# A hybrid decoder layer: x laid out by columns for the Z stage, unscaled fp32 products first, and roots spread by TensorE

## The chip, the cores and the metric

The kernel runs on one core of a Trainium2 chip. A core has five engines that run side by side, each through its own list of instructions in order: TensorE (PE in the profile; its weight loads are PEld), VectorE (DVE), ScalarE (ACT), GpSimd (POOL) and SyncE (SP), which here only starts transfers between the device memory and the on-chip memory. Matrix products land in eight accumulator banks (PSUM), from which VectorE and ScalarE read. The metric is the device time of one execution in microseconds. Three runs are shown for the kernel before; a further execution was recorded by the profiler.

## The reference, cut to what matters

One decoder layer on x of 1024 tokens by 1024 features, all in float32. The part that the change touches is the first norm and the last 520 columns of the input projection: the gate z (512 columns) and the two small inputs a and b of the delta rule (8 columns).

```python
def rms_norm(x, w):
    y = x * lax.rsqrt(jnp.mean(x * x, axis=-1, keepdims=True) + EPS)
    return y * w

h = rms_norm(x, norm1_w)
proj = h @ w_in
da_q, da_k, da_v, dn_qkv, dn_z, dn_a, dn_b = jnp.split(proj, [...], axis=-1)
...
dn_o = rms_norm(dn_o, dn_out_norm_w) * jax.nn.silu(dn_z)
...
x = x + mix @ w_out
h = rms_norm(x, norm2_w)
x = x + jnp.square(jax.nn.relu(h @ w_up)) @ w_down
```

The root of a token (one over the root mean square of its row of x) scales a whole row of h. So it can be put on a row of the product as well: (r x) W = r (x W).

## The kernel before, in words

The kernel keeps h turned, that is with features over partitions and tokens along the free axis, because a product contracts over partitions. It keeps it as two float32r tensors: `hH`, the rounded value, and `hL`, what the rounding left. A product of full precision is made of three passes of float32r (H by H, H by L, L by H); I call it a split product.

The Z stage is the first of the kernel, up to 63 us. It has eight blocks of 128 tokens and two units of 260 columns of weights (u = 0 and 1), so 16 products. For a block `tb` the steps before are:

- `z_square` (ScalarE): squares of a row of x (tokens over partitions), summed along the way; `z_root`: mean and epsilon on VectorE (L223), power -1/2 on GpSimd (L224);
- `z_scale` (L335, VectorE): x times root times norm weight, rows as they came;
- `z_turn` (L340, TensorE): eight 128 by 128 transposes into two banks;
- `h_round` (L345, ScalarE) writes `hH` out of the banks and `h_rest` (L349, VectorE) writes `hL`;
- `z_mm` (L290 to L292, TensorE): the split product with a unit, 24 matmuls of 260 columns;
- `z_gate`: tanh (L298, ScalarE), (tanh + 1) times z (L300, VectorE), times the norm weight of the gated output (L301, GpSimd), and a store from SyncE's queue (L304); the second unit also yields the eight columns a and b (L303).

The weights arrive as float32 (`wraw`) and are split by `z_round` (L308, ScalarE) and `z_rest` (L312, VectorE). The very first product, block 0 with unit 0, is made in plain fp32 from an unsplit copy `hF` (L388), since nothing is split yet. The norm weight is spread over all partitions by two products with a row of ones (L362) and copied out (L366, L369). Ahead of and between these stand twelve transposes that nobody reads (L358, L365).

Order: inside `tc.manual_schedule(engines={T, V, S})` (L352) TensorE, VectorE and ScalarE run the instructions in the order in which the program writes them. GpSimd and SyncE are ordered by a planner that simulates the program. The loop at L421 runs over blocks 2 to 7: the first product of the block, turns and splits of the next block, the gate, square, root and scaling of the block after that, the second product and its gate. What follows the stage in the text (masks, small constants, L441 to L507) is planned to issue behind the instructions collected in `mark` and the last load of x. All loads and the stores of gates go through SyncE's one queue, in order: block 0 of x in halves, block 1, the eight pieces of weights of both units, the gate's norm weight, blocks 2 to 7 of x, then the small constants and the first weights of the next stage (`load_unit`, L191).

After the Z stage come the delta rule's projections (`dn_proj`, first product at L198), the scan, attention, the output projection and the MLP. Their order on TensorE is fixed by the program.

## Time and profile before

| | us |
|---|---|
| median of 3 runs | 1255.41 |
| lowest, highest | 1255.33, 1256.09 |
| the profiled execution | 1254.91 |
| its span | 1253.2 |
| TensorE, VectorE, ScalarE, GpSimd busy | 1232.7, 817.7, 612.5, 111.4 |

The granted clock of TensorE was 0.997 over the span.

How to read the profile: all times are microseconds from the start of the span unless a row says ns. A row of the timeline has start, duration, engine, source line, operation, output<-inputs, shapes, count, and in brackets the idle time ahead of it and what ended it. A group's row ends with busy time and mean duration in ns, then the idle time before its instructions by what ended it. The chain of waits is the chain of work that ended last, followed back from the end; its rows have start, duration, engine, tile and line. A row of waits on SyncE's queue names the line that waited, what for, the total, the times and the longest. Matmuls are pipelined, so a matmul is booked longer than the distance to the next.

### The profile page before, as it was taken

The numbers are of one execution on the slowest core, as the hardware profiler recorded it, in microseconds if no ns is written. First come the engines' busy times: TensorE is split into PE (matmuls) and PEld (weight loads), VectorE is DVE, ScalarE is ACT, GpSimd is POOL, SyncE is SP. The second block draws the span as 40 slices with busy tenths as digits, with TensorE's granted clock in tenths as the row PEclk, the third lists the DMA queues.
The fourth block names the chain that finished last, engine by engine and source line by source line (L and its number), as shares of the span: only waits on it lengthen the run. The fifth ranks groups of instructions, "written<-read, shape, count | busy, mean of one in ns | idle before, by whom it ended". The sixth has DMA issues, their size and how long they took to land.

```text
span 1253.2 us, 18946 instructions
## 1 busy us (share of the span) xinstructions
PE 1232.7 (98%) x6965; PEld 1061.6 (85%) x6965; DVE 817.7 (65%) x1416; ACT 612.5 (49%) x1239; POOL 111.4 (9%) x143
## 2 busy tenths in 40 slices
PE   9999999999998999999999999999999999999998
PEld 8978888899998998787888888888888888888887
DVE  6567797656556647776589555655569855787553
ACT  5378553334345545656567445445564333333331
POOL 3311110022112200001200000000000000000000
PEclk9999999999999999999999999999999999999999
DMA  7134554368758557322255544443469655422301
GB/s 245 43 102 129 160 159 113 89 215 240 249 144 243 157 176 180 97 66 80 85 185 172 201 159 175 168 152 132 170 219 376 230 199 201 168 101 101 133 35 67
DMA packets 156343, 197.93 MB, mean 158 GB/s; under 512 B 20650, under 2 KB 110554, under 8 KB 156251
## 3 DMA queue, kind: packets, MB, share of 16 engines
q1 hardware_dynamic: 156248, 196.72, 48.4%
q8 instruction: 55, 0.90, 0.3%
q14 instruction: 38, 0.30, 0.1%
q10 hardware_dynamic: 2, 0.00, 0.0%
HBM read 131.66 MB, written 65.01 MB: 157 GB/s over the span
## 4 chain that ended last, share of the span: by engine, by line
PE 91%; DMA 4%; DVE 2%; ACT 2%; issue 1%; SPq 0%; DVEq 0%; POOL 0%; ACTq 0%; POOLq 0%
PE X L1391 5%; PE X L1392 5%; PE X L1393 5%; PE X L1691 4%; PE X L1690 4%; PE X L1689 4%; PE ps_dn L198 3%; PE ps_dn L199 3%; PE ps_dn L200 3%; PE ps_qk L955 3%; PE ps_qk L957 3%; PE ps_qk L956 3%; PE Y L1391 2%; PE Y L1392 2%; PE Y L1393 2%; PE ps_op L1220 2%
## 5 line engine op out<-in xcount | busy, mean ns | idle before, releaser
L1309 ACT CAST hH<-ur 128x1024 fp32r<-128x1024 f32 x56 | 58.9, 1051 | 173.3 <-PE Y L1690 89.8
L1310 DVE TENSOR_TENSOR hL<-ur,hH 128x1024 fp32r<-128x1024 f32 x56 | 68.3, 1223 | 79.9 <-ACT hH L1309 79.8
L955 PE MATMUL ps_qk<-wH,hH 128*128 128x256 f32 x384 | 115.5, 301 | 0.1
L957 PE MATMUL ps_qk<-wH,hL 128*128 128x256 f32 x384 | 109.1, 284 | 0.0
L956 PE MATMUL ps_qk<-wL,hH 128*128 128x256 f32 x384 | 109.0, 284 | 0.0
L1310 DVE TENSOR_TENSOR op<-raw,op 128x1024 fp32r<-128x1024 f32 x48 | 58.7, 1223 | 74.5 <-PE X L1392 41.5
L1689 PE MATMUL X<-hH 128*128 128x512 f32 x224 | 87.1, 389 | 0.0
L1690 PE MATMUL X<-hL,hH 128*128 128x512 f32 x224 | 87.1, 389 | 0.0
L1691 PE MATMUL X<-hH,hL 128*128 128x512 f32 x224 | 87.1, 389 | 0.0
L198 PE MATMUL ps_dn<-hH,wH 128*128 128x512 f32 x192 | 76.1, 397 | 0.3 <-ACT cp L574 0.3
L200 PE MATMUL ps_dn<-hH,wL 128*128 128x512 f32 x192 | 75.9, 396 | 0.0
L199 PE MATMUL ps_dn<-hL,wH 128*128 128x512 f32 x192 | 75.7, 395 | 0.0
L955 PEld LDWEIGHTS ps_qk<-wH,hH 128*128 128x128 f32 x384 | 74.0, 193 | 0.3 <-ACT qn L974 0.2
L956 PEld LDWEIGHTS ps_qk<-wL,hH 128*128 128x128 f32 x384 | 74.0, 193 | 0.0
L957 PEld LDWEIGHTS ps_qk<-wH,hL 128*128 128x128 f32 x384 | 73.8, 192 | 0.0
L193 DVE TENSOR_TENSOR wL<-wraw,wH 128x512 fp32r<-128x512 f32 x64 | 43.9, 697 | 37.9 <-ACT wH L192 37.7
L1310 DVE TENSOR_TENSOR hL<-dw,hH 128x1024 fp32r<-128x1024 f32 x56 | 68.1, 1219 | 0.5 <-ACT hH L1309 0.5
L1309 ACT CAST op<-raw 128x1024 fp32r<-128x1024 f32 x48 | 50.4, 1051 | 35.3 <-PE Y L1393 19.9
L1309 ACT CAST hH<-dw 128x1024 fp32r<-128x1024 f32 x56 | 58.7, 1048 | 10.1 <-DMA dw<-in_w_down_dram 4.4
L192 ACT CAST wH<-wraw 128x512 fp32r<-128x512 f32 x64 | 38.2, 620 | 48.7 <-DMA wraw<-in_w_units_dram 35.3
L578 DVE SCALAR_TENSOR_TENSOR cy<-cp,pv,cy 128x512 f32<-128x512 f32 x72 | 53.7, 747 | 7.2 <-ACT cy L576 6.4
L1080 DVE TENSOR_REDUCE mx<-ps_sc 128x1 f32<-128x128 f32 (+7 forms) x64 | 47.6, 754 | 15.3 <-PE ps_sc L1078 14.8
(366 smaller groups left out, 3451.3 us busy)
## 6 DMA issues: line engine op xcount, KB each, us to landing
ur<-ud SPq DMA_DIRECT2D x28, 1024.0 KB, 4.9
raw<-in_w_up_dram SPq DMA_DIRECT2D x32, 512.0 KB, 4.1
dw<-in_w_down_dram SPq DMA_DIRECT2D x32, 512.0 KB, 6.6
wraw<-in_w_units_dram SPq DMA_DIRECT2D x48, 256.0 KB, 3.9
qk_d<-qa SPq DMA_DIRECT2D x32, 256.0 KB, 3.6
ud<-ua SPq DMA_DIRECT2D x16, 512.0 KB, 3.3
ud<-s SPq DMA_DIRECT2D x16, 512.0 KB, 2.7
pka<-park_d SPq DMA_DIRECT2D x32, 192.0 KB, 3.7
```

What stands on the lines that cost most here:

```text
L198: T.matmul(ps, lh(k), rh(k), start=(k == 0), stop=False)
L199: T.matmul(ps, lh(k), rl(k), start=False, stop=False)
L200: T.matmul(ps, ll(k), rh(k), start=False, stop=(k == n - 1))
L955: T.matmul(ps[:, :256], hH[:, k, sl], wh[:, k, :], start=(k == 0), stop=False)
L956: T.matmul(ps[:, :256], hH[:, k, sl], wl[:, k, :], start=False, stop=False)
L957: T.matmul(ps[:, :256], hL[:, k, sl], wh[:, k, :], start=False, stop=(k == KB - 1))
L1309: S.copy(dst[0], src)
L1310: V.tensor_tensor(dst[1], src, dst[0].bitcast(F32), ALU.subtract)
L1391: T.matmul(ps, op[0][:, k, cs], h[0][:, k, :], start=start and k == 0, stop=False, skip_group_check=True)
L1689: T.matmul(bank[t], v[0][:, j, sl], v[2][:, j], start=s0, stop=False, skip_group_check=True)
L1690: T.matmul(bank[t], v[0][:, j, sl], v[3][:, j], start=False, stop=False, skip_group_check=True)
L1691: T.matmul(bank[t], v[1][:, j, sl], v[2][:, j], start=False, stop=s1, skip_group_check=True)
```

## The change

The host passes two more arrays: `x_cols`, x with each block of 128 tokens turned (features over partitions), and `w1_cols`, the norm weight in the same layout. x itself is still loaded, as rows, for the squares alone.

- A block of columns `xT` is weighed in place with the norm weight (`z_weigh`): blocks 0 and 1 on VectorE, blocks 2 to 7 on GpSimd, in two halves.
- The four products of blocks 0 and 1 (`z_raw`) are plain fp32 products of weighed but unscaled columns with unsplit weights. Their gates take the root as a scale: half the root inside the tanh, and the root in a second step on VectorE, which also multiplies by the gate's norm weight; that step was GpSimd's.
- A root is still a value per token on a partition. To scale columns, it has to lie along the free axis, the same on all partitions. `z_diag` puts the roots on a diagonal (VectorE), `z_spread` multiplies a matrix of ones by it (TensorE, fp32, 128 columns), and the result in a bank is multiplied onto `xT` by `z_scale` (VectorE, two halves). `hH` and `hL` are then made from `xT` in the on-chip memory.
- A spread stands inside a product, after its first two of eight steps: that of block 2 in the last unscaled product, of 3 in the first product of block 2, of 0 in the second product of block 2, of 4 in the first product of block 3, of 1 in the second of block 3, and then of each block in the first product of the one before.
- Blocks 0 and 1 are scaled and split late, after block 3, since only later stages read them.
- GpSimd now also runs in the written order. Its masks are written ahead of the stage. The transposes of normed rows, the broadcast of the norm weight and the copy `hF` are gone; ten transposes that nobody reads stand at the start.
- Tiles: six for `xT`, four for rows of x, one for squares, two for diagonals. Loads: half of `xT` 0, a piece of weights, the other half, three pieces, `xT` 1, four pieces, then `xT` and x of blocks 2 and 3, the gate's norm weight, x of blocks 0 and 1, and `xT` and x of blocks 4 to 7.

The diff, cut to its core:

```diff
+    def z_raw(tb, u, pool, tag, mid=None):
+
+        ps = pool.tile([P, 512], F32, tag=tag, name="ps_z")
+        for k in range(KB):
+            if k == 2 and mid is not None:
+                z_spread(mid)
+            T.matmul(ps[:, :UC], xTs[tb][:, k, :], wz[u][1][k // 2][:, k % 2, :], start=k == 0, stop=k == KB - 1)
+        return ps
+
+    def z_gate(tb, u, ps, raw=False):
         n = UC if u == 0 else 252
         th = n1.tile([P, UC], F32, tag="zth", name="zth", bufs=2)
-        S.activation(th[:, :n], ps[:, :n], AF.Tanh, scale=0.5)
         zg = n1.tile([P, UC], F32, tag="zg", name="zg", bufs=4)
+        r = roots[tb]
+        S.activation(th[:, :n], ps[:, :n], AF.Tanh, scale=half_r[tb] if raw else 0.5)
         last = V.scalar_tensor_tensor(zg[:, :n], th[:, :n], 1.0, ps[:, :n], ALU.add, ALU.mult)
-        G.tensor_tensor(zg[:, :n], zg[:, :n], dnw4[:, UC * u:UC * u + n], ALU.mult)
-        if u == 1:
+        w = dnw4[:, UC * u:UC * u + n]
+        if raw:
+            last = V.scalar_tensor_tensor(zg[:, :n], zg[:, :n], r, w, ALU.mult, ALU.mult)
+        else:
+            G.tensor_tensor(zg[:, :n], zg[:, :n], w, ALU.mult)
+        if u == 1 and raw:
+            last = V.tensor_scalar(ab[:, tb, :], ps[:, 252:260], r, None, ALU.mult)
+        elif u == 1:
             last = V.tensor_copy(ab[:, tb, :], ps[:, 252:260])
...
+    roots, half_r, spreads, diags = {}, {}, {}, {}
+
+    def z_weigh(tb, eng, parts=2):
         for i in range(parts):
+            c = cuts[i] if parts > 1 else slice(0, KB)
+            n = KB // parts
+            eng.tensor_tensor(xTs[tb][:, c, :], xTs[tb][:, c, :],
+                              w1c[:, c].unsqueeze(2).broadcast_to([P, n, P]), ALU.mult)
+
+    def z_root(tb):
+
+        sq = n1.tile([P, DM], F32, tag="sq", name="sq", bufs=1)
+        ss = n1.tile([P, 1], F32, tag="nss", name="nss", bufs=2)
+        S.activation(sq, xts[tb], AF.Square, accum_out=ss)
+        r = roots[tb] = n1.tile([P, 1], F32, name=f"nr{tb}")
+        rstd(r, ss, 1.0 / DM, EPS, n1, "nrt", 1)
+
+    def z_diag(tb):
+        diags[tb] = n1.tile([P, P], F32, tag="dg", name="dg", bufs=2)
+        V.tensor_scalar(diags[tb], ident, roots[tb], None, ALU.mult)
+
+    def z_spread(tb):
+
+        ps = pm.tile([P, 512], F32, tag="pm", name="ps_r")
+        marks[tb] = T.matmul(ps[:, :P], ones, diags[tb], start=True, stop=True)
+        spreads[tb] = ps[:, :P]
+
+    def z_scale(tb):
+        sl = slice(tb * P, (tb + 1) * P)
+        xT, last = xTs[tb], []
+        for c in cuts:
+            V.tensor_tensor(xT[:, c, :], xT[:, c, :], spreads[tb].unsqueeze(1).broadcast_to([P, 4, P]), ALU.mult)
+            last.append(S.copy(hH[:, c, sl], xT[:, c, :]))
+        for c in cuts:
+            last.append(V.tensor_tensor(hL[:, c, sl], xT[:, c, :], hH[:, c, sl].bitcast(F32), ALU.subtract))
         return last
...
+        for i in range(10):
             T.transpose(pw[:, 0:P], ident, ident)
+        z_weigh(0, V)
+        z = {(0, 0): z_raw(0, 0, pj, "pj")}
+        for i in range(3):
             z_round(0, i)
             z_rest(0, i)
+        z_weigh(1, V)
+        z_round(0, 3)
+        z_rest(0, 3)
+        z[1, 0] = z_raw(1, 0, pj, "pj")
+        for i in range(4):
             z_round(1, i)
             z_rest(1, i)
+        z[0, 1] = z_raw(0, 1, ph, "ph")
+        z_weigh(2, G)
         z_root(2)
+        z_diag(2)
+        z_weigh(3, G)
+        z[1, 1] = z_raw(1, 1, ph, "ph", 2)
+        z_scale(2)
         z_root(3)
+        z_diag(3)
+        z[2, 0] = z_mm(2, 0, pt_, "pt", 3)
+        G.tensor_scalar(dnw4[:, 0], dnw4[:, 0], 0.5, None, ALU.mult)
+        G.tensor_copy(dnw4[:, 1:4], dnw4[:, 0:1].broadcast_to([P, 3, P]))
+        dnw4 = dnw4.rearrange("p h e -> p (h e)")
+        for tb in range(2):
+            z_root(tb)
+            half_r[tb] = n1.tile([P, 1], F32, name=f"hr{tb}")
+            V.tensor_scalar(half_r[tb], roots[tb], 0.5, None, ALU.mult)
+            z_diag(tb)
+            if tb == 0:
+                z_scale(3)
+            for u in range(2):
+                z_gate(tb, u, z[tb, u], True)
+            if tb == 0:
+                z[2, 1] = z_mm(2, 1, pt_, "pt", 0)
+                z_weigh(4, G)
+        z_gate(2, 0, z[2, 0])
+        z_scale(0)
+        z_root(4)
+        z_diag(4)
+        for tb in range(3, NT):
+            z[tb, 0] = z_mm(tb, 0, mid=tb + 1 if tb + 1 < NT else None)
+            if tb + 2 < NT:
+                z_weigh(tb + 2, G)
             if tb + 1 < NT:
+                last = z_scale(tb + 1)
+            z_gate(tb - 1, 1, z[tb - 1, 1])
+            if tb == 3:
+                mark = [marks[4], *last]
+            z[tb, 1] = z_mm(tb, 1, mid=1 if tb == 3 else None)
+            if tb == 3:
+                z_scale(1)
+            z_gate(tb, 0, z[tb, 0])
             if tb + 2 < NT:
                 z_root(tb + 2)
+                z_diag(tb + 2)
+        z_gate(NT - 1, 1, z[NT - 1, 1])
```

More of the change, by code (lines that the diff above doesn't have):

```diff
@@ L252, in tile_hymba_layer, with z_unit @@
     ab = const.tile([P, NT, 8], F32, name="ab")
[L253 to L255 removed]
+    def z_unit():
         ops = [staged(t).rearrange("p (k c) -> p k c", k=KB) for t in ("wH", "wL")]
@@ L344, in h_round @@
[L344 to L355 removed]
+            c = cuts[i] if parts > 1 else slice(0, KB)
@@ L356, in tile_hymba_layer @@
+    G.affine_select(gt_f, ones, pattern=[[-1, P]], compare_op=ALU.is_gt, fill=0.0,
+                    base=0, channel_multiplier=1)
+    G.affine_select(blk.rearrange("p (b c) -> p b c", c=32), ones.rearrange("p (b c) -> p b c", c=32),
+                    pattern=[[-32, 4], [0, 32]], compare_op=ALU.is_ge, fill=0.0,
+                    base=-32, channel_multiplier=1)
+    marks = {}
+    with tc.manual_schedule(engines={T.engine, V.engine, S.engine, G.engine}):
         pw = pm.tile([P, 512], F32, tag="pm", name="ps_w")
-        for i in range(6):
+        for i in range(10):
```

182 lines of the change are left out of this document (48 added, 134 removed).

## The prediction

> **What bounds the kernel now.** I read the page first: the span and the busy time of each engine.
>
> ```profile
> span 1253.2 us, 18946 instructions
> PE 1232.7 (98%) x6965; PEld 1061.6 (85%) x6965; DVE 817.7 (65%) x1416; ACT 612.5 (49%) x1239; POOL 111.4 (9%) x143
> ```
>
> TensorE (PE) is busy for 98% of the span, so time can only come out of its work, or out of the first microseconds; and every microsecond in which it newly waits is lost. The change touches only the Z stage. So next came the chain of waits from 0 to 66 us, and TensorE's timeline for the stage's first and last products.
>
> ```profile
> 10.20 1.96 PE ps_z L388 x8
> 13.03 1.75 PE ps_z L388 x8
> 40.90 0.87 PE ps_tr L340 x8
> 47.52 0.87 PE ps_tr L340 x8
> 24.26 0.29 PE L290 MATMUL ps_z<-wH,hH 128*128 128x260 f32 x1
> 63.45 0.40 PE L198 MATMUL ps_dn<-hH,wH 128*128 128x512 f32 x1
> ```
>
> The chain is TensorE throughout. The one fp32 product (L388) has 16 records in 1.96 + 1.75 = 3.7 us. A block of 128 tokens lasts 47.52 - 40.90 = 6.62 us; less 0.87 us for the eight turns (L340) that leaves 5.75 us for two split products, 2.87 us each. At about 24.3 us the four products of blocks 0 and 1 are done and block 2 is turned; at 63.45 us the next stage begins. In between lie 12 split products (34.4 us), five groups of turns (4.35 us) and one small turn with the joints (0.4 us): 39.15 us, without a wait. VectorE (DVE), ScalarE (ACT) and GpSimd (POOL) are hidden under it.
>
> **The change, part by part: the front.** The first product needs no root, no scaling and no turning any more. It needs half a block of x by columns, w1_cols, one weighing instruction on VectorE and the first piece of weights. How fast pieces land is read from the queue of SyncE.
>
> ```profile
> 3.54 0.63 ACT L321 ACTIVATE hn<-xt 128x512 f32<-128x512 f32 x1 [0.90 <-DMA xt<-in_x_dram]
> 7.49 1.06 ACT L321 ACTIVATE hn<-xt 128x1024 f32<-128x1024 f32 x1 [2.61 <-DMA xt<-in_x_dram]
> 8.20 0.33 SPq L275 DMA_DIRECT2D dnw<-in_dn_out_norm_w_dram  x1
> 8.85 3.73 SPq L277 DMA_DIRECT2D xt<-in_x_dram  x6
> SPq L277 <- DMA wraw<-in_w_z_dram: 1.9, 6, 0.3
> ```
>
> The first 0.26 MB are there at 3.5 us, 1.05 MB at 7.5 us. The issue at 8.20 us and the six from 8.85 us each waited for a piece of weights, one 0.27 MB piece per 0.67 us (0.40 MB/us). Read on this scale, with an early end about 1 us ahead of it because the first pieces are smaller, the changed order lands half a block at 3.5 us, the first weights at 4.2 us, the second weight piece (1.06 MB in all) at 6.5 to 7.5 us, the fourth (1.6 MB) at 8 to 8.9 us, block 1 (2.1 MB) at 9.3 to 10.2 us, the last weights (3.2 MB) at 12 to 12.9 us. So the first product starts at about 4.3 us but is paced by weights; the second waits for block 1 and half its weighing (0.7 us) until 10.0 to 10.9 us. From there the products run on: three at 3.7 us and one spread, so four are done at 21.3 to 22.2 us. I take 21.8 us: 2.5 us ahead of 24.3 us. The 4.2 MB of x that are now loaded twice add 10.5 us of traffic at this rate. Behind them on SyncE's queue stand the small constants and the first two pieces of unit weights:
>
> ```profile
> 12.87 0.45 SPq L464 DMA_DIRECT2D rows<-in_conv_w_dram  x1
> 24.21 0.90 SPq L191 DMA_DIRECT2D wraw<-in_w_units_dram  x2
> 36.53 0.22 DVE L443 CAST identb<-ident 128x128 bf16<-128x128 f32 x1
> 61.06 1.13 ACT L192 CAST wH<-wraw 128x512 fp32r<-128x512 f32 x2
> ```
>
> They went out at 12.9 to 25 us and were used from 36 us (constants) and 61 us (unit weights). They move behind the last x, whose slot comes free when block 1 is scaled, at about 42 us; eleven issues at 0.45 us and two of weights then end near 48 us. I cost this at nothing: some 12 us of products still cover the unit weights. Without that cover ScalarE would wait for a landing, and the next stage's first product with it.
>
> **TensorE's work after that.** The five groups of turns go (-4.35 us); six spreads come. A spread is one fp32 product of 128 columns in two records; eight one-record turns took 0.87 us, so two records are about 0.22 us, 0.25 us with the change of operands: +1.5 us. From 21.8 us TensorE has 34.4 + 1.5 = 35.9 us. With the 0.4 us of small turn and joints, and without a wait, the stage would end at 58.1 us, 5.35 us earlier than before.
>
> **The waits that come.** The roots no longer scale rows ahead of the turns; each block now goes square (ACT), mean (DVE), power (POOL), diagonal (DVE), spread (PE), two scalings (DVE), two roundings (ACT), two rests (DVE). All four engines run in the order written. The spread of block 4 stands inside the first product of block 3, after six of its matmuls; but its diagonal stands on VectorE behind the scaling of block 3, the gates of blocks 0 and 1, one gate of block 2 and the whole scaling of block 0. The durations, from the groups of the Z stage (0 to 63.4 us), of GpSimd over the whole kernel, and the timeline:
>
> ```profile
> L349 DVE TENSOR_TENSOR hL<-ps_tr,hH 128x512 fp32r<-128x512 f32 x14 | 9.0, 687 | 10.8 <-ACT hH L345 10.8
> L300 DVE SCALAR_TENSOR_TENSOR zg<-zth,ps_z 128x260 f32<-128x260 f32 x8 | 3.3, 417 | 2.6 <-ACT zth L298 2.4 <-DMA zg_d<-zg 0.2
> L321 ACT ACTIVATE hn<-xt 128x1024 f32<-128x1024 f32 x7 | 7.5, 1066 | 2.6 <-DMA xt<-in_x_dram 2.6
> L345 ACT CAST hH<-ps_tr 128x512 fp32r<-128x512 f32 x14 | 7.5, 589 | 17.4 <-PE ps_tr L340 17.4
> L224 POOL TENSOR_TENSOR nr<-nrt,neghalf 128x1 f32<-128x1 f32 x8 | 4.4, 552 | 9.7 <-DVE nrt L223 9.1 <-DVE qw L473 0.7
> L1249 POOL TENSOR_TENSOR hn<-hn,w2b 128x512 f32<-128x512 f32 x4 | 5.2, 1290 | 5.5 <-ACT hn L1248 5.5
> 45.03 1.28 DVE L335 SCALAR_TENSOR_TENSOR hn<-xt,nr,w1b 128x1024 f32<-128x1024 f32 x1 [1.08 <-POOL nr L224]
> 46.24 0.41 DVE L300 SCALAR_TENSOR_TENSOR zg<-zth,ps_z 128x252 f32<-128x252 f32 x1
> 37.82 0.21 DVE L490 TENSOR_SCALAR dawb<-dawb 128x128 f32<-128x128 f32 x1
> ```
>
> One instruction follows another 0.07 us before the first is booked as ended (45.03 + 1.28 against 46.24), so a half-block pass costs VectorE 0.62 us, a gate step 0.34 us, a diagonal 0.2 us.
>
> Block 3's root comes first. The spread of block 2 is issued at about 18.3 us; two scalings and two roundings end at 20.5 us; the square of block 3 (1.07 us and 0.1 us of reading) follows on ScalarE, then mean, power (0.55 us) and diagonal, ready at 22.8 us (times on the early bound of the front). TensorE stands at that spread from 22.05 us: 0.8 us lost.
>
> From 22.8 us VectorE's list to the diagonal of block 4 is: three means, two half roots and three diagonals (1.1 us), the scaling and rests of blocks 3 and 0 (8 x 0.62 = 5.0 us), nine gate steps (3.1 us), two small copies (0.24 us): 9.4 us. It also waits, with nothing else in its order, for the power of block 0 (its square queues behind that of block 3: 1.3 us), the power of block 1 (0.7 us), a tanh (0.25 us), the square of block 4 behind block 0's roundings (0.6 us) and its power (0.7 us): 3.55 us. So the diagonal is ready at about 35.8 us. TensorE reaches the spread at 29.1 us: after 22.85 us it has the rest of one split product (0.25 + 2.1 us), one with a spread (3.1 us) and 0.7 us. It loses 6.8 us.
>
> Block 5 is next: between the two spreads VectorE has the scaling of blocks 4 and 1 and two gates, 6.1 us and 1.5 us of waits, against 6.0 us of TensorE work: 1.8 us lost. From block 6 on the list is one scaling and two gates per 5.98 us of TensorE, and it fits. Sum of the waits: 9.4 us.
>
> **GpSimd's new passes.** Weighing blocks 2 to 7 puts two 1.29 us passes per block on GpSimd. What they do to VectorE is shown by four meetings in the timeline.
>
> ```profile
> 24.09 1.27 DVE L335 SCALAR_TENSOR_TENSOR hn<-xt,nr,w1b 128x1024 f32<-128x1024 f32 x1
> 24.18 2.47 POOL L301 TENSOR_TENSOR zg<-zg,dnw 128x252 f32<-128x252 f32 x2 [1.46 <-DVE ab L303]
> 25.29 0.41 DVE L300 SCALAR_TENSOR_TENSOR zg<-zth,ps_z 128x252 f32<-128x252 f32 x1
> 36.75 0.75 POOL L301 TENSOR_TENSOR zg<-zg,dnw 128x260 f32<-128x260 f32 x1 [2.52 <-issue]
> 36.80 0.78 DVE L461 CAST caus<-caus_f 128x128 bf16<-128x128 f32 x1
> 61.71 1.85 DVE L193 TENSOR_TENSOR wL<-wraw,wH 128x512 fp32r<-128x512 f32 x2
> 61.76 1.24 POOL L301 TENSOR_TENSOR zg<-zg,dnw 128x260 f32<-128x260 f32 x1 [2.16 <-issue]
> ```
>
> Each time the later one stood until the earlier had ended: GpSimd's pair took 2.47 us instead of 1.45 us behind L335; the cast took 0.78 us instead of 0.22 us; L193 and GpSimd took turns. L300, which reads one input from PSUM, was not held. In the changed lists a weighing is issued on GpSimd straight behind the power, and the diagonal of the same block (SBUF to SBUF, like the cast) a hop later. So the diagonals of blocks 0, 4, 5 and 6 each stand behind a 1.29 us pass, and so do some rests. Lower bound 0, upper bound four times 1.23 us, 4.9 us; I take 4.8 us, since every meeting on record held.
>
> The Trainium skill, "SBUF — State Buffer", section "Who interferes with whom", has the rule: VectorE and GpSimd share one port pair that whoever issues first keeps for the whole instruction, and VectorE needs it for two SBUF inputs or for a two-port copy, cast or tensor_scalar. By that rule the sum is the one with 4.8 us, without it the one with 0; the four rows agree with it.
>
> Other edits. The gates of blocks 0 and 1 move their last multiply to VectorE (counted above). VectorE's constants (L443 to L490) still have to lie somewhere behind the scaling of block 4; 0 to 2.0 us, and I take 0, the value that the timeline of before shows. The warm-up at the start has two transposes fewer and no broadcast of the norm weights; all of it lies ahead of the first product.
>
> **Sum.** -2.5 us (front), -2.85 us (turns less spreads), +9.4 us (waits), +4.8 us (passes): +8.85 us; the stage ends at 72.3 us, and what follows, with TensorE as full as before, moves by the same. The profiled execution took 1254.9 us (span 1253.2 us), 0.5 us under the median of the runs shown, 1255.4 us; so about 1263.8 us. Below 0.2% (2.5 us) a measurement of this kernel can't tell a change from none.
>
> **Rivals.**
> A, not slower: VectorE's list runs without hand-over waits and without standing behind GpSimd. Then its 9.4 us alone count: diagonal 4 at 32.2 us, 3 us lost there, 0.8 us at block 3, none at block 5. The sum is -5.35 + 3.8 = -1.55 us, 1253.4 us; with the front's early bound 1252.9 us. It decides once all waits together stay under 5.35 us. For it: VectorE was busy for only 65%. Against: the hand-overs follow from the written order, and L335 already waited 1.08 us for a power.
> B, the passes cost nothing: -5.35 + 9.4 = +4.05 us, 1259 us. For it: no pass as wide as these meets VectorE in the Z stage of before. Against: the four rows.
> C, TensorE slows after its long wait. At the start it ran at half rate:
>
> ```profile
> 1.53 1.54 PE L358 MATMUL ps_w<-ident 128*128 128x128 f32 x6 [1.53 <-POOL ident masks.py:199]
> 11.99 1.04 PE L340 MATMUL ps_tr<-ident,hn 128*128 128x128 f32 x8
> ```
>
> Six transposes took 1.54 us early and eight 1.04 us later, 0.22 against 0.11 us apiece. If it falls back after standing for 7 to 9 us, some 3.6 us of work cost double: +1.9 us, 1265.7 us; as long as at the start (from 1.5 to 10.4 us) up to +4.4 us, 1268.2 us. Nothing before shows a wait that long. The Trainium skill, "TensorE: Matmul & The Clock Gate", Part 1, says an idle window of about 3.4 us halves the clock until as much sustained work has passed; by an estimate from that page it is the +1.9 us.
> D, the constants land in the blocks where VectorE's list is the limit: +2.0 us, 1265.8 us.
>
> **Chances.** The forecast (1261 to 1265.5 us) 0.48; A 0.15, of which 0.09 at or past its early end (faster) and 0.06 short of it (same); B 0.17; C 0.12; D 0.08. The range leaves out A: 1257 to 1269 us, from 2 us under B to past the far end of C. Faster 0.09, same 0.06, slower 0.85.
>
> **What would show it.** Right: the first Z product before 5 us; the fourth done at 21 to 22.5 us; TensorE waiting 5 to 9 us at the fourth spread, that of block 4, near 29 us; a diagonal booked with over 1 us beside a weighing; the next stage's first L198-type product at 67 to 74 us. Wrong: that product before 63 us, or a spread of block 4 that hardly waits, which would mean that VectorE's order is not the limit; or a later stage that takes the delay up.

## The result and the profile after

The changed kernel takes 1269.3 us (median of four runs, 1266.95 to 1271.39), the kernel before 1255.5 us on the same chip: 1.0109 times as long, interval 1.0087 to 1.013. The forecast was 1263.8 us, with a range of 1257 to 1269 us: slower was right, but the time lies 5.5 us above the forecast and 0.3 us above the range. The profiled execution took 1267.9 us.

From the page of the changed kernel, the lines that answer to the first ones of before:

```profile
span 1266.2 us, 18837 instructions
PE 1229.3 (97%) x6887; PEld 1058.6 (84%) x6887; DVE 827.0 (65%) x1438; ACT 614.1 (49%) x1235; POOL 119.5 (9%) x151
PEclk9799999999999999999999999999999999999999
```

TensorE has 3.4 us less work than before and the span is 13.0 us longer, so it stands still for some 16 us more. The second slice of 32 us is the only one in which the granted clock is under nine tenths. Its timeline shows the places; the number in brackets is the time without work ahead of the row and what ended it.

```profile
4.86 0.77 PE L322 MATMUL ps_z<-wraw,xT 128*128 128x260 f32 x1 [0.93 <-DMA wraw<-in_w_z_dram]
21.58 0.47 PE L311 MATMUL ps_z<-wH,hH 128*128 128x260 f32 x1
23.64 0.35 PE L375 MATMUL ps_r<-dg,ones 128*128 128x128 f32 x1 [1.00 <-DVE dg L370]
40.60 0.55 PE L375 MATMUL ps_r<-dg,ones 128*128 128x128 f32 x1 [10.55 <-DVE dg L370]
49.03 0.39 PE L311 MATMUL ps_z<-wH,hH 128*128 128x260 f32 x1 [0.87 <-DVE qw L490]
51.53 0.55 PE L375 MATMUL ps_r<-dg,ones 128*128 128x128 f32 x1 [1.52 <-DVE dg L370]
62.85 0.36 PE L311 MATMUL ps_z<-wH,hH 128*128 128x260 f32 x1 [1.11 <-DVE ab L340]
70.16 0.36 PE L311 MATMUL ps_z<-wH,hH 128*128 128x260 f32 x1 [1.11 <-DVE ab L340]
78.83 0.39 PE L198 MATMUL ps_dn<-hH,wH 128*128 128x512 f32 x1
```

The first product starts at 4.86 us and the first scaled one (block 2, unit 0) at 21.58 us. From there the stage lasts 78.83 - 21.58 = 57.25 us; I call this the scaled stretch and compare the experiments by it, since the start of the first scaled product differs by up to 1.8 us between profiles. Six waits, 16.2 us together, lie in it. The longest is the one at the spread of block 4. What VectorE did meanwhile:

```profile
23.18 0.31 DVE L370 TENSOR_SCALAR dg<-ident,nr 128x128 f32<-128x128 f32 x1 [0.67 <-POOL nr L224]
24.80 0.15 DVE L438 TENSOR_SCALAR hr<-nr 128x1 f32<-128x1 f32 x1 [1.11 <-POOL nr L224]
24.88 0.99 DVE L370 TENSOR_SCALAR dg<-ident,nr 128x128 f32<-128x128 f32 x1
31.00 0.15 DVE L438 TENSOR_SCALAR hr<-nr 128x1 f32<-128x1 f32 x1 [0.66 <-POOL nr L224]
31.75 0.42 DVE L331 SCALAR_TENSOR_TENSOR zg<-zth,ps_z 128x260 f32<-128x260 f32 x1 [0.41 <-ACT zth L330]
35.23 0.42 DVE L331 SCALAR_TENSOR_TENSOR zg<-zth,ps_z 128x260 f32<-128x260 f32 x1 [1.54 <-DMA zg_d<-zg]
38.58 0.15 DVE L223 TENSOR_SCALAR nrt<-nss 128x1 f32<-128x1 f32 x1 [0.36 <-ACT sq L364]
39.40 1.05 DVE L370 TENSOR_SCALAR dg<-ident,nr 128x128 f32<-128x128 f32 x1 [0.66 <-POOL nr L224]
```

Between the diagonals of block 3 (23.18 us) and block 4 (booked until 40.45 us) VectorE works through blocks 3, 0 and 1, and itself stands still for 4.7 us: for GpSimd's roots, a tanh, a square, and for 1.54 us at gate(2,0), whose buffer `zg` still waits for a store. Two of the diagonals take 0.99 and 1.05 us instead of 0.31 us. Behind the long wait TensorE is slow (windows; the columns behind the busy times are granted clock, DMA share and GB/s):

```profile
30.00:40.00 10.00, 0.05 (x1) 0.00 (x0) 6.21 (x17) 3.49 (x7) 2.47 (x4) 0.70 0.54 176
40.00:44.00 4.00, 3.40 (x16) 3.43 (x17) 2.96 (x6) 1.59 (x4) 1.37 (x2) 0.50 0.15 33
50.00:55.00 5.00, 3.48 (x19) 3.50 (x19) 3.62 (x6) 1.50 (x3) 2.30 (x3) 0.66 0.08 27
55.00:78.80 23.80, 21.52 (x177) 20.98 (x176) 11.72 (x27) 8.01 (x17) 9.36 (x12) 1.00 0.12 41
```

From 41.0 to 44.3 us and from 52.0 to 54.6 us the matmuls follow each other at 0.217 us instead of 0.12 us, which with the two slow spreads costs about 3.1 us. The stage ends 15.4 us later than before (78.8 against 63.45 us); at the end of the span 13.0 us of that are left.

### The profile page after: what moved, and what is told of

Same layout as the page of the kernel before. It is cut to its first block, busy times and chain, and to the rows that moved or that the text cites. A ratio compares the mean times of both kernels' runs of the same rounds, so it can differ in the third digit from the quotient of the medians.

```text
span 1266.2 us, 18837 instructions
## 1 busy us (share of the span) xinstructions
PE 1229.3 (97%) x6887; PEld 1058.6 (84%) x6887; DVE 827.0 (65%) x1438; ACT 614.1 (49%) x1235; POOL 119.5 (9%) x151
## 4 chain that ended last, share of the span: by engine, by line
PE 87%; DMA 6%; DVE 3%; ACT 2%; issue 1%; SPq 0%; POOL 0%; DVEq 0%; ACTq 0%; POOLq 0%
PE X L1410 5%; PE X L1409 5%; PE X L1408 5%; PE X L1706 4%; PE X L1708 4%; PE X L1707 4%; PE ps_dn L198 3%; PE ps_dn L199 3%; PE ps_dn L200 3%; DMA wraw<-in_w_units_dram 3%; PE ps_qk L972 3%; PE ps_qk L973 3%; PE ps_qk L974 3%; PE Y L1408 2%; PE Y L1409 2%; PE Y L1410 2%
## 5 line engine op out<-in xcount | busy, mean ns | idle before, releaser
L1327 DVE TENSOR_TENSOR op<-raw,op 128x1024 fp32r<-128x1024 f32 x48 | 58.7, 1223 | 73.8 <-PE X L1409 40.8
L198 PE MATMUL ps_dn<-hH,wH 128*128 128x512 f32 x192 | 76.1, 397 | 0.3 <-ACT cp L591 0.3
L1101 ACT ACTIVATE pexp<-ps_sc,mx 128x128 f32<-128x128 f32 (+7 forms) x64 | 47.3, 741 | 19.8 <-DVE mx L1097 19.4
```

The costliest lines, as they stand in the source:

```text
L198: T.matmul(ps, lh(k), rh(k), start=(k == 0), stop=False)
L1327: V.tensor_tensor(dst[1], src, dst[0].bitcast(F32), ALU.subtract)
```

## The experiments

Ratios are to the kernel before; the changed kernel's is 1.0109. The intervals of the single mends (e1 to e4, e6 to e8, e12) all overlap the changed kernel's, so by their times they cannot be told from it; what is said of them rests on one profiled execution each. "Stretch" is the scaled stretch of that execution, 57.25 us in the changed kernel.

**e1: no weighing on GpSimd.**

```diff
-            eng.tensor_tensor(xTs[tb][:, c, :], xTs[tb][:, c, :],
-                              w1c[:, c].unsqueeze(2).broadcast_to([P, n, P]), ALU.mult)
+            if tb < 2:
+                eng.tensor_tensor(xTs[tb][:, c, :], xTs[tb][:, c, :],
+                                  w1c[:, c].unsqueeze(2).broadcast_to([P, n, P]), ALU.mult)
```

> The twelve GpSimd passes that weigh the columns of blocks 2 to 7 with the norm weight are left out (these columns then lack that weight; nothing else changes). Theory one, GpSimd's passes hold VectorE: in the changed kernel the diagonals took 0.99 to 1.05 us beside such a pass and 0.28 to 0.31 us alone, so they fall to about 0.3 us everywhere, VectorE's list gets 4 to 5 us shorter, and the Z stage ends 3 to 5 us sooner than in the changed kernel (at 74 to 76 us instead of 78.8). Theory two, the long diagonals are another engine's doing (they wait for their root and the record only starts early): they stay near 1 us and the Z stage ends within 1 us of the changed kernel's.

Stretch 55.3 us (22.26 to 77.54 us), ratio 1.0098 (1.0077 to 1.0119). From its timeline, the diagonals of blocks 0, 1 and 4, a gate, and the spread of block 4; below, all waits of TensorE in the stretch (what waited, for what, total, times, longest):

```profile
25.56 0.28 DVE L371 TENSOR_SCALAR dg<-ident,nr 128x128 f32<-128x128 f32 x1
31.05 0.28 DVE L371 TENSOR_SCALAR dg<-ident,nr 128x128 f32<-128x128 f32 x1
39.50 0.29 DVE L371 TENSOR_SCALAR dg<-ident,nr 128x128 f32<-128x128 f32 x1 [0.66 <-POOL nr L224]
35.33 0.43 DVE L331 SCALAR_TENSOR_TENSOR zg<-zth,ps_z 128x260 f32<-128x260 f32 x1 [1.67 <-DMA zg_d<-zg]
39.93 0.55 PE L376 MATMUL ps_r<-dg,ones 128*128 128x128 f32 x1 [9.20 <-DVE dg L371]
```

```profile
PE ps_r L376 <- DVE dg L371: 11.0, 3, 9.2
PE ps_z L311 <- DVE ab L340: 3.3, 3, 1.1
PE ps_z L311 <- DVE qw L491: 0.9, 1, 0.9
```

The mechanism stands: without a pass beside them the diagonals take 0.28 us. But all passes together are worth 2.0 us of the stretch, not 4.8 us, and only 1.0 us of that is waits (15.2 instead of 16.2 us). Most of the rest, some 1.3 us, is the second spell at half rate, which does not come here: the granted clock is 1.00 from 45 to 55 us. The spread of block 4 comes 1.35 us sooner (17.67 instead of 19.02 us after the first scaled product), about two held diagonals; 9.2 us of the wait stay.

**e2: root of block 4 ahead.**

```diff
+        z_root(4)
+        z_diag(4)
         z_gate(2, 0, z[2, 0])
         z_scale(0)
-        z_root(4)
-        z_diag(4)
```

> The root and the diagonal of block 4 are moved ahead of gate(2,0) and scale(0) in the order of VectorE and ScalarE. Theory one, VectorE's list is too long and the wait of 10.5 us is only the place where it shows: the wait at the spread of block 4 falls to 4 to 6 us, but some 3 us come back as a new wait at the first product of block 4, so the Z stage ends only 1 to 2 us sooner (77 to 78 us). Theory two, only the place of the root in the order was wrong: the wait falls by 4 to 6 us and the stage end falls by all of it (73 to 75 us).

```profile
34.26 0.58 PE L375 MATMUL ps_r<-dg,ones 128*128 128x128 f32 x1 [4.69 <-DVE dg L370]
46.18 0.40 PE L311 MATMUL ps_z<-wH,hH 128*128 128x260 f32 x1 [3.60 <-DVE zg L331]
```

The wait at the spread falls by 5.9 us, and a new one of 3.6 us stands at the first product of block 4. Stretch 55.5 us (-1.8), ratio 1.0103 (1.008 to 1.0126). Theory one: one place mended, the delay shows at the next.

**e3: PSUM buffers in turn.**

```diff
-            z[tb, 0] = z_mm(tb, 0, mid=tb + 1 if tb + 1 < NT else None)
+            pb = (pt_, "pt") if tb % 2 == 0 else (pj, "pj")
+            z[tb, 0] = z_mm(tb, 0, *pb, mid=tb + 1 if tb + 1 < NT else None)
...
-            z[tb, 1] = z_mm(tb, 1, mid=1 if tb == 3 else None)
+            z[tb, 1] = z_mm(tb, 1, *pb, mid=1 if tb == 3 else None)
```

> The products of even blocks from 4 on go into the two PSUM buffers that blocks 2 and the second products of blocks 0 and 1 leave free, those of odd blocks stay in the two of before. Theory one, the waits of TensorE at 49.0, 62.9 and 70.2 us are waits for a PSUM buffer that a gate standing behind a scaling still reads: these three vanish (0.9 + 1.1 + 1.1 us, with the half us around each), and the Z stage ends 2 to 3.5 us sooner. Theory two, the gates are late because VectorE is, and the wait only moves to the next scaled block: the three waits are replaced by waits at the weight-bearing products or at spreads of equal length, and the stage end moves by less than 0.7 us.

```profile
39.96 0.55 PE L375 MATMUL ps_r<-dg,ones 128*128 128x128 f32 x1 [11.04 <-DVE dg L370]
51.68 0.35 PE L375 MATMUL ps_r<-dg,ones 128*128 128x128 f32 x1 [2.54 <-DVE dg L370]
```

All three waits for a buffer are gone, as theory one says, but the waits at the two spreads are 1.5 us longer: stretch 55.9 us (-1.4), below the 2 us that I expected. Ratio 1.0085 (1.006 to 1.0109).

**e4 and e8: TensorE kept busy through the wait.**

```diff
         ps = pm.tile([P, 512], F32, tag="pm", name="ps_r")
+        for _ in range({4: 98, 5: 14}.get(tb, 0)):
+            T.transpose(ps[:, P:2 * P], ident, ident)
```

This is e8; e4 has 80 ahead of the spread of block 4 and none ahead of that of block 5.

> Eighty transposes of the identity into an unused part of the spread's own PSUM tile are put ahead of the spread of block 4, in the place where TensorE stood for 10.5 us. Theory one, TensorE's clock falls during that wait and costs 1.5 to 2 us behind it: the products behind the spread run at 0.11 us each from the first, and the Z stage ends 1.3 to 2 us sooner. Theory two, the slow products there wait for something else (their data, the records are uneven): they still take 0.2 us each, and the stage end moves by less than 0.5 us.

> The changed kernel with 98 transposes of the identity ahead of the spread of block 4 and 14 ahead of that of block 5, so that TensorE works through both waits and not only through most of the first. Theory one, the half rate behind these waits is the clock's answer to idle time: the products behind both spreads run at 0.12 us each, the wait of 2.0 us that was left with 80 transposes is gone, and the stretch from the first scaled product to the end of the Z stage falls by 1.5 to 3 us against the changed kernel's 57.2. Theory two, VectorE sets the pace of these blocks at any clock: the rate is full but the waits behind grow by as much, and that stretch stays within 1 us.

In e4 the 80 transposes took 8.9 us; a wait of 2.03 us was left and the half rate followed it all the same, so it does not tell the theories apart. Small constants moved on VectorE too, and the first product of block 4 waited 1.9 us instead of 0.9 us: stretch 59.2 us, ratio 1.0137 (1.0114 to 1.0159). In e8 both waits are filled. Its windows:

```profile
40.00:44.00 4.00, 4.00 (x36) 4.00 (x35) 3.51 (x11) 1.59 (x4) 0.64 (x1) 1.00 0.04 3
50.00:55.00 5.00, 3.89 (x31) 3.60 (x30) 3.54 (x9) 2.91 (x6) 2.25 (x3) 1.00 0.01 2
```

The clock is full throughout, so the half rate is the answer to TensorE's idle time (theory one). But the stretch falls by 1.1 us only, to 56.15 us (ratio 1.0092, 1.0064 to 1.0119), which lies between the ranges of the two theories: waits of 1.9 us at block 4 and 1.1 us at the second product of block 4 stand in the place of those of 0.9 and 1.5 us. The spread of block 4 comes 19.0 us after the first scaled product, as in the changed kernel: VectorE sets the pace there at either clock.

**e6 and e7: more buffers for gates; diagonals on ScalarE.**

```diff
-        zg = n1.tile([P, UC], F32, tag="zg", name="zg", bufs=4)
+        zg = n1.tile([P, UC], F32, tag="zg", name="zg", bufs=8)
```

```diff
-        V.tensor_scalar(diags[tb], ident, roots[tb], None, ALU.mult)
+        S.activation(diags[tb], ident, AF.Copy, scale=roots[tb])
```

> The gated products get eight buffers instead of four; nothing else changes. Theory one, VectorE's wait of 1.5 us for a store of a gated product lies inside TensorE's wait of 10.5 us: it vanishes, TensorE's wait falls by 1.2 to 1.6 us and the Z stage ends 1 to 1.6 us sooner. Theory two, what waits there is covered by the next wait in the list (the root of block 4, or the load of x): TensorE's wait stays within 0.5 us.

> The diagonals of the roots are written by ScalarE instead of VectorE; nothing else changes. Theory one, a diagonal costs its time and its hold by GpSimd's passes on VectorE, 0.7 to 1.0 us of VectorE's list for each, while ScalarE writes it in about 0.3 us beside those passes: TensorE's wait at the spread of block 4 falls by 1.5 to 3 us and the Z stage ends 2 to 4 us sooner. Theory two, the list is held by the waits for GpSimd's root and not by the diagonals: they only move to ScalarE, and the Z stage ends within 1 us of the changed kernel's.

The spread of block 4 in e6, then in e7:

```profile
38.03 0.55 PE L375 MATMUL ps_r<-dg,ones 128*128 128x128 f32 x1 [8.92 <-DVE dg L370]
```

```profile
39.95 0.58 PE L375 MATMUL ps_r<-dg,ones 128*128 128x128 f32 x1 [10.38 <-ACT dg L370]
```

e6: the wait for the store is gone, TensorE's falls by 1.6 us, the stretch by 1.2 us to 56.0 us (ratio 1.0115, 1.0095 to 1.0135). That wait was on the path. e7: TensorE's wait falls by 0.2 us, the stretch by 0.3 us to 56.9 us (ratio 1.0104, 1.0088 to 1.012). Theory two: the diagonal waits for GpSimd's root on ScalarE just as long.

**e12: constants later** (collected behind block 7 instead of block 4).

```diff
-            if tb == 3:
-                mark = [marks[4], *last]
+            if tb == 6:
+                mark = [marks[7], *last]
```

> The changed kernel with the small constants issued behind the scaling of block 7 instead of block 4. In the changed kernel some 1.9 us of VectorE's time between 43.9 and 49.1 us is theirs, and the wait of 0.9 us at the first product of block 4 ends behind one of them. Theory one, they land where VectorE's list is the limit (rival D): the waits at block 4 and at the spread of block 5 fall by 1 to 2 us together and the stretch from the first scaled product to the end of the Z stage falls from 57.2 to 55.2 to 56.2 us. Theory two, they fill time in which VectorE waits for the root of block 5 anyway: that stretch stays within 0.6 us.

The waits are 1.00, 10.50, 0.95, 1.53, 1.09 and 1.43 us, the stretch 57.7 us (+0.5), the ratio 1.0091 (1.0064 to 1.0119). Theory two: VectorE's constants cost nothing in the changed kernel.

Up to here no single mend was worth over 2.0 us, though most did to their own wait what they should. (e7 and e12, which took no wait away, moved the stretch by -0.3 and +0.5 us.) That left the order as a whole.

**e5: the same work in another order.**

```diff
+        at = {2: {6: 3}, 6: {2: 7}, 7: {2: 1}}
+        for tb in range(2, NT):
+            z[tb, 0] = z_mm(tb, 0, at.get(tb, {4: tb + 1}))
+            nx, old, up = tb + 2, tb - 4, tb + 1 if tb + 1 < NT else 1
+            if nx < NT:
+                z_weigh(nx, G)
+                z_square(nx)
+            if old in (0, 1):
+                z_square(old)
+            if tb > 2:
+                z_gate(tb - 1, 1, z[tb - 1, 1])
+            last = z_scale(up)
+            if nx < NT:
+                z_root(nx)
+            last += z_low(up)
+            if old in (0, 1):
+                z_root(old)
+            if tb == 6:
+                mark = [marks[up], *last]
+            z[tb, 1] = z_mm(tb, 1, {2: 0} if tb == 6 else {})
+            if nx < NT:
+                z_diag(nx)
+            z_gate(tb, 0, z[tb, 0])
+            if old in (0, 1):
+                half_r[old] = n1.tile([P, 1], F32, name=f"hr{old}")
+                V.tensor_scalar(half_r[old], roots[old], 0.5, None, ALU.mult)
+                z_diag(old)
+            if tb == 5:
+                for u in range(2):
+                    z_gate(0, u, z[0, u], True)
+            if tb == 6:
+                z_scale(0)
+                z_low(0)
+        z_gate(NT - 1, 1, z[NT - 1, 1])
+        for u in range(2):
+            z_gate(1, u, z[1, u], True)
```

Here `nx` is the block to be prepared, `old` is block 0 or 1, `z_square` (the square) is taken out of `z_root` and `z_low` (the rests) out of `z_scale`, `at` puts a spread at another step of the product, all scaled products use the two buffers `pt_`, there are four diagonals, x by columns of blocks 6 and 7 takes the buffers of the unsplit weights, x of blocks 0 and 1 is loaded last, and the small constants wait for the scaling of block 7, as in e12.

> The arithmetic of the changed kernel in another order. The gates, roots and scalings of blocks 0 and 1 go behind those of blocks 4 to 7 on every engine, each gate of a product stands ahead of the scaling that its PSUM buffer waited behind, each square, root and diagonal is issued half a block or more before it is needed, the small constants come two blocks later; x by columns of blocks 6 and 7 takes the buffers of the unscaled weights, so that nothing waits for block 0's. Theory one, the waits of the Z stage are waits on the order of VectorE's list (work of blocks 0 and 1 that nothing needs soon, and small operations that stand still for GpSimd's root), not on its amount of work: TensorE has no wait over 1 us from the first scaled product on, the Z stage ends at 57 to 62 us (78.8 in the changed kernel, 63.5 in the kernel before), and the time is 1249 to 1255 us. Theory two, VectorE, with GpSimd's passes beside it, has too much work for TensorE's pace: the waits come back in other places, the stage ends at 68 us or later, and the time is above 1258 us.

```profile
span 1247.8 us, 18833 instructions
21.53 0.47 PE L316 MATMUL ps_z<-wH,hH 128*128 128x260 f32 x1
58.44 0.40 PE L198 MATMUL ps_dn<-hH,wH 128*128 128x512 f32 x1
```

Stretch 36.9 us, without a single wait of TensorE in it. The time is 1249.4 us, ratio 0.9959 (0.9945 to 0.9974): faster than both kernels. Theory one holds: VectorE's work and GpSimd's passes are the same as in the changed kernel (1438 and 151 instructions in both) and fit beside TensorE's; 20.3 us were lost to their order, with the buffers and loads that go with it. Not all of VectorE's work lies in the stretch any more: the gates of block 1 run from 61.6 to 64.0 us, behind the stage's end, and VectorE is busy for 29.5 us of the stretch instead of 35.5 us.

**e9, e10, e11, e13, e14: which part of the order.** Each is e5 with something put back: e9 the gate of a second product behind the scaling; e10 square, root and diagonal together at the end of a block; e14 both of these; e11 the work of blocks 0 and 1 into blocks 2 to 4, with their loads of x ahead; e13 the same with x of blocks 4 and 5 loaded first.

The edit of e9 and e14, then the core of that of e10 and e14, then that of e11 and e13:

```diff
-            if tb > 2:
-                z_gate(tb - 1, 1, z[tb - 1, 1])
             last = z_scale(up)
...
             last += z_low(up)
+            if tb > 2:
+                z_gate(tb - 1, 1, z[tb - 1, 1])
```

```diff
             if tb == 5:
                 for u in range(2):
                     z_gate(0, u, z[0, u], True)
+            if nx < NT:
+                z_square(nx)
+                z_root(nx)
+                z_diag(nx)
```

```diff
-            nx, old, up = tb + 2, tb - 4, tb + 1 if tb + 1 < NT else 1
+            nx, old, up = tb + 2, tb - 2, tb + 1
...
-            z[tb, 1] = z_mm(tb, 1, {2: 0} if tb == 6 else {})
+            z[tb, 1] = z_mm(tb, 1, {2: tb - 3} if tb in (3, 4) else {})
+            if tb in (3, 4):
+                z_scale(tb - 3)
+                z_low(tb - 3)
```

> The reordered kernel with one thing put back: the gate of a block's second product stands behind the scaling and the rest of the next block again. Theory one, this alone keeps TensorE waiting for a PSUM buffer once in every block: a wait of 1 to 2 us at the second product of each block, some of them followed by the half rate, and the Z stage ends 6 to 12 us later than in the reordered kernel (64 to 70 us). Theory two, the buffers are freed in time once VectorE has no work of blocks 0 and 1 ahead: no wait over 0.5 us, end within 1 us.

> The reordered kernel with one thing put back: square, root and diagonal of a block are issued together at the end of the block two ahead, as in the changed kernel, so that VectorE stands still for ScalarE's square and GpSimd's root. Theory one, the chain square, root, diagonal costs 2 to 2.5 us of standing still each time and TensorE waits 1 to 2.5 us at some of the spreads: the Z stage ends 3 to 7 us later than in the reordered kernel (61 to 65 us). Theory two, with the work of blocks 0 and 1 gone from the list there is room for the chain: end within 1 us.

> The reordered kernel with one thing put back: roots, gates and scalings of blocks 0 and 1 are issued during blocks 2 to 4 (and x of blocks 0 and 1 is loaded before x of block 4). Theory one, this work is what TensorE waited for at the spread of block 4: waits of 1 to 3 us come back in blocks 3 to 5 and the Z stage ends 4 to 10 us later than in the reordered kernel (62 to 68 us). Theory two, the place of this work does not matter while gates and diagonals stand early in the list: end within 1.5 us.

> The kernel with the work of blocks 0 and 1 early again, but with x of blocks 4 and 5 loaded ahead of x of blocks 0 and 1, so that no square waits for a load. Theory one, the early work itself holds TensorE: the wait of 6.7 us at the first product of block 3 shrinks to 1 to 3 us, waits of 1 to 3 us stay in blocks 3 to 5, and the stretch from the first scaled product to the end of the stage is 42 to 48 us (36.9 in the reordered kernel, 52.5 with the late load). Theory two, nearly all was the late load of x of block 4: that stretch is under 40 us.

> The reordered kernel with both other things put back at once: gates behind the scaling, and square, root and diagonal together at the end of a block; of the three changes of order only the late work of blocks 0 and 1 is left. Theory one, that change is the largest: the stretch from the first scaled product to the end of the stage is 45 to 48 us, so that it alone takes 9 to 12 of the 20.4 us. Theory two, the three only help together: the stretch is above 52 us.

| kernel | stretch, us | ratio to before |
|---|---|---|
| e5 | 36.9 | 0.9959 (0.9945 to 0.9974) |
| e9, gates behind the scaling | 44.75 | 1.0049 (1.0032 to 1.0066) |
| e10, late roots | 42.0 | 0.9985 (0.9971 to 1.0) |
| e13, early work of blocks 0 and 1 | 44.6 | 1.0016 (1.0 to 1.0031) |
| e11, the same with the load late | 52.55 | 1.0055 (1.0036 to 1.0073) |
| e14, gates behind and late roots | 45.7 | 1.0057 (1.004 to 1.0074) |

(e9 and e14 are taken to the end of the last split product, since the next stage's first product waited 1.0 us for its own weights there.) The waits of TensorE in the stretch, as the view of waits gives them: e9, then e10, then e13.

```profile
PE ps_z L316 <- DVE nrt L223: 3.6, 2, 1.8
PE ps_z L316 <- DVE ab L345: 3.3, 2, 1.8
```

```profile
PE ps_r L383 <- DVE dg L378: 4.5, 3, 2.7
```

```profile
PE ps_z L316 <- DVE hr L478: 2.3, 1, 2.3
PE ps_z L316 <- DVE zg L336: 2.2, 1, 2.2
PE ps_z L316 <- DVE ab L345: 2.0, 2, 1.4
```

Each of the three alone brings waits back, as theory one says of e9, e10 and e13. e11 missed both of its theories: its stage ended at 73.8 us. In it a square stood 7.4 us for the load of block 4, which made 8 us of its loss; that confounded it, and e13 tells them apart: the early work itself is 7.7 us, with the other two mends in place. Taken one after the other from the changed kernel: late work of blocks 0 and 1 57.25 to 45.7 us (e14, 11.5 us), gates ahead 45.7 to 42.0 us (e10), early roots 42.0 to 36.9 us (e5). The 11.5 us hold all else that e14 shares with e5 (PSUM buffers, four diagonals, later spreads, loads, constants), so no run here gives the late work's own share of the way from the changed kernel. The stretches also hold spells at half rate: two in e9, one in e14, none in e5, e10 and e13.

## Why the prediction was right in sign and too low

The mechanism and most of the places were as forecast; what failed is the size of three terms of the sum. "The waits that come" stood at 9.4 us, while e1, in which no pass runs, has 15.2 us of waits. The half rate behind a long wait (rival C) stood at nothing, though the sum itself held a wait of 9 us; it took 3.1 us. "GpSimd's new passes" stood at 4.8 us and were worth 2.0 us. The third error hid about half of the first: that waits and passes together came to 16.2 us against 14.2 us forecast is partly luck.

| step of the prediction | forecast, us | measured, us |
|---|---|---|
| first scaled product | 21.8 | 21.58 |
| scaled stretch without waits | 36.3 | 36.9 (e5) |
| wait at the spread of block 3 | 0.8 | 1.00 |
| wait at that of block 4, with two held diagonals | 6.8 + 2.4 | 10.55 |
| block 5, with one held diagonal | 1.8 + 1.2 | 0.87 + 1.52 |
| later blocks | 1.2 | 1.11 + 1.11 |
| half rate behind the waits | 0 (rival C: 1.9) | 3.1 |
| end of the stage | 72.3 | 78.83 |
| taken up later | 0 | -2.4 |

The stage ended 6.5 us later than forecast: 2.0 us of it are waits (16.2 instead of 14.2 us), 3.1 us the half rate, the rest the joints behind each wait (0.16 us) and in the products. Less the 2.4 us taken up later that is 4.1 us, by which the profiled execution (1267.9 us) lies above 1263.8 us. The median lies 1.4 us higher still; the forecast was added up from the profiled execution of before, not from the median. Of the signs named ahead, the wait at the spread of block 4 (10.55 us, 5 to 9 forecast) and the first L198 product (78.83 us, 67 to 74 forecast) lay past their ranges, both on the side of the miss.

**Front and turns less spreads.** Right. Without waits these steps gave a stage end of 58.1 us and 1254.9 - 2.5 - 2.85 = 1249.55 us; e5, which has no waits in the stretch, ended the stage at 58.44 us and took 1249.4 us (the kernel before, run beside it, 1254.2 us).

**"The waits that come"**: the mechanism was right, and so were the places up to block 5; the size was too small, for three reasons. First, VectorE's list to the diagonal of block 4 left out the wait of 1.54 us for a store at gate(2,0); e6 shows that it was on the path. Second, "from block 6 on the list is one scaling and two gates ... and it fits" counted the list's length and not what its order does to PSUM buffers: the second product of a block needs the buffer that a gate behind the next scaling still reads. That is 1.11 us in each of blocks 5 and 6 and part of the 0.87 us of block 4; e3 shows it. Third, the two steps of an unscaled gate took 0.85 us (28.36 to 29.21 in the rows below), not twice 0.34 us: 0.7 us for four of them.

```profile
28.36 0.42 DVE L331 SCALAR_TENSOR_TENSOR zg<-zth,ps_z 128x260 f32<-128x260 f32 x1
28.81 0.49 DVE L334 SCALAR_TENSOR_TENSOR zg<-zg,nr,dnw 128x260 f32<-128x260 f32 x1
29.21 0.41 DVE L331 SCALAR_TENSOR_TENSOR zg<-zth,ps_z 128x252 f32<-128x252 f32 x1
```

**"GpSimd's new passes".** The hold is shown (e1), but the term was too large. A pass takes 1.02 us, not 1.29 us (row below, two passes in 2.04 us), a held diagonal loses 0.7 us, and all passes together are worth 2.0 us, of which 1.0 us is waits. I priced each meeting at full length and as if it lay on the path.

```profile
24.74 2.04 POOL L357 TENSOR_TENSOR xT<-xT,w1c 128x512 f32<-128x512 f32 x2
```

**Rivals.** A (VectorE's list runs dense) did not happen, and e5 shows what it would have needed. B (the passes cost nothing) is refuted by e1 as to the hold, though its price was nearer. C happened: TensorE fell to half rate, behind two waits and not one, 3.1 us against my 1.9 us. It should have been in the sum, since the sum itself had a wait of 9 us; but e8 shows that taking it out gains 1.1 us only. D (constants in the limited blocks) is half right: they do land there, and e12 shows that they cost nothing.

**What follows the stage.** The shift of 15.4 us at the stage's end was 13.0 us at the end. In the fourteen variants the difference between the two (shift of the span less shift of the first L198) lies anywhere from -4.4 us (e10) to +3.3 us (e14), so I read no fixed step from it. What takes it up is open.

## What to carry to other kernels

In-order lists have to be costed by what stands behind what, and not by their sums: the same instructions took 57 or 37 us from the first scaled product to the next stage. Before pricing a new operation, ask at each point of an engine's list which instruction stands still for another engine, which buffer the next product needs, and which work there nobody will need soon; put such work at the end. When each single mend returns under a tenth of the loss, as here, the wait has only moved, and the mends have to be made together.

## What the runs showed of the hardware

TensorE's clock falls to half after waits shorter than the 7 to 9 us that I had in mind. In e9 a wait of 1.82 us that ended at 32.75 us, with none over 0.3 us in the 5 us before it, was enough; its windows:

```profile
32.00:34.00 2.00, 1.25 (x7) 1.28 (x8) 1.13 (x5) 1.97 (x4) 1.40 (x3) 0.81 0.13 39
34.00:36.00 2.00, 2.00 (x11) 2.00 (x11) 0.00 (x0) 0.25 (x2) 2.00 (x3) 0.50 0.17 44
36.00:38.00 2.00, 2.00 (x16) 2.00 (x16) 0.00 (x0) 0.00 (x0) 0.09 (x1) 0.84 0.52 147
```

What is missing of the granted clock, 0.19, 0.50 and 0.16 of 2 us each, is 1.7 us, or 3.4 us at half rate. Of the six waits of 1.8 us in e9 and e14 three were followed by it, each for 3.4 us; one wait of 2.7 us (e10) and two of 2.3 us (e13) were not, and waits of 1.1 us alone never were. So the length of a wait does not decide it by itself. The Trainium skill, "TensorE: Matmul & The Clock Gate", Part 1, says that an idle window of about 3.4 us halves the clock and that the window runs free of the kernel. The 3.4 us at half rate agree with that length; that 1.8 us of standing can be enough does not agree with a wholly idle window.

The runs show how such a wait decides it. In eleven of the profiled executions the granted clock changes between 15 and 82 us. (Earlier its column reads 1.00 even where ten transposes take 2.39 us, from 1.53 us on in the changed kernel, so that part is left out.) Windows of 0.2 us give the moments; three of the changed kernel, each with a change in it:

```profile
33.80:34.00 0.20, 0.00 (x0) 0.00 (x0) 0.00 (x0) 0.00 (x0) 0.00 (x0) 0.98 0.66 243
44.20:44.40 0.20, 0.20 (x3) 0.20 (x3) 0.20 (x4) 0.00 (x0) 0.00 (x0) 0.92 0.00 0
51.00:51.20 0.20, 0.00 (x0) 0.00 (x0) 0.20 (x1) 0.00 (x0) 0.20 (x1) 0.65 0.29 89
```

A mean of 0.98 between full and half rate puts the fall at 33.99 us; likewise the rise lies at 44.23 us, the next fall at 51.06 us and the next rise at 54.47 us. Within each of the eleven executions all changes lie whole multiples of 3.41 us apart, to 0.02 us. So a grid of 3.41 us can be laid over each, and TensorE's idle time (a wait, and the 0.16 us by which the matmul ahead of it is booked too long) summed up in each cell of the grid:

| execution, cell, us | idle | clock at the cell's end |
|---|---|---|
| e9, 29.82 to 33.24 | 1.98 us, 58% | falls |
| e9, 50.30 to 53.72 | 1.55 us, 45% | stays full |
| e14, 38.93 to 42.34 | 1.98 us, 58% | falls |
| e14, 49.16 to 52.58 | 1.63 us, 48% | stays full |
| e1, 47.98 to 51.40 | 1.74 us, 51% | stays full |
| changed kernel, 47.64 to 51.06 | 2.25 us, 66% | falls |

At full rate the clock fell at the end of all 20 cells that were idle for 58% or more, and of none of the 148 that were idle for 51% or less. At half rate it rose at the end of all 20 cells idle for 14% or less, and of none of the 18 idle for 19% or more. So a cell need not be wholly idle: a wait of 1.8 us halves the clock when it falls into one cell and does not when it is split over two. The grid lies elsewhere in each execution, so a spell at half rate, up to 1.7 us lost, can come or not by chance, and single stretches that differ by as much are to be read with that in mind. Where the border lies between 51 and 58% is open, and for e10 and e13, whose clock never changes, no grid can be laid.
